# First tap and silu of the latents' convolutions: from VectorE and an exp/ln sigmoid to ScalarE and tanh

## The chip, the cores and the metric

The kernel runs on one core of one Trainium2 chip. The metric is the device time of one execution in microseconds (us). Three runs of the kernel before took 3646.48, 3650.38 and 3652.74 us; their median is 3650.38 us. Five engines work beside each other, each through its own queue in order: TensorE (PE for matmuls, PEld for its weight loads), VectorE (DVE), ScalarE (ACT), GpSimd (POOL), and SyncE (SP), whose queue issues most DMAs. An instruction that waits for a semaphore holds up everything that stands behind it in its queue.

## What is computed

The program is two blocks one after the other on a sequence of 1024 tokens of width 1024: a first block of two layers (dilated attention with a gated scan, then a second gated scan), and a second block with a hybrid mixer and an expert layer. The change lies in the hybrid mixer of the second block, on its 1024 latent tokens. What matters of the reference:

```
def dwconv_centred(u, w):          # width 5, one filter per channel
    ...
def ssd_stream(z, xbc, ...):
    xbc = jax.nn.silu(dwconv_centred(xbc, conv_w) + conv_b)
    ...
    y = y.reshape(b, T, SSD_DIM) * jax.nn.silu(z)
    return rms_norm(y, norm_g), s_f, s_b

def gdn_stream(qkv, gate, ...):
    qkv = jax.nn.silu(dwconv_centred(qkv, conv_w))
    q, k, v = ...
    q = l2_norm(q) * (GDN_HEAD_DIM ** -0.5)
    k = l2_norm(k)
    ...
    o = rms_norm(o_f + flip_t(o_b), norm_g) * jax.nn.silu(gate)
```

So there are 16 blocks of 128 channels that are projected, convolved and put through silu: three each of k, q and v (the delta rule, "gdn", in column-major token order), and seven of xbc (the state-space branch, "ssd", which alone has a bias). k and q are normalised per head afterwards. Six more blocks are gates: projected and put through silu, without a convolution. The same code also handles 256 context tokens earlier in the program, with `lat` false.

## The kernel before

The latents' stage (`latent_mixers`) holds 128 channels on the partitions and 1024 tokens along the free dimension. For each block, `Projections.dense` loads the weights, splits them into a high and a low part (`whi` by ACT, L115, and `wlo` by POOL, L116) and multiplies in two halves of 512 tokens, 24 matmuls each (`mm3`, L139 to L141), into one of three PSUM banks `mm`.

`Projections.conv` then does, for each of the 16 blocks: two copies from PSUM into the padded tile `cu` (ACT, L1134 or L1137); the first tap (DVE, L1141, or L1143 with the bias); four more taps (DVE, L1145); the silu as `sigmoid` (L612 exp on ACT, L613 a clamp on DVE, L614 ln and L615 exp on ACT) and a product (DVE, L1148). The sigmoid is written over `cu`. For q and k there follow a square (ACT, L1150), a sum over each head by a matmul (L1153), and per half a scale (DVE, L1156), ln and exp (ACT, L1157 and L1158) and a product (DVE, L1159). At last the result `cacc` is stored by a DMA that SP issues (L1160). `cu`, `cacc` and the scale `cr` have two buffers each, so the first tap of a block waits until the block two before has been stored.

`Projections.gate` does the six gate blocks with `silu_from`: exp, clamp, ln, exp and a product on each half of 512 tokens, straight from PSUM.

Beside this runs `gdn_inverse`, three generators (one for each pair of heads) that invert triangular matrices. Its core is a recursion of 31 steps of two DVE instructions each (`gtmp` L1465 and `gTT` L1466), a POOL copy (`gN`, L1470), DMAs through DRAM, and small matmuls (`a`, L1504 to L1514). The loop over the blocks draws four steps of it after each block. Three k blocks come first, then q and v alternately, then the seven xbc blocks x0 to x6, the six gates, and a pooling branch (`pu`). When the last inverse is stored, the next stage (the two scans) begins with loads on SP (L1228 to L1595).

The order of instructions on each engine is not written out by hand: the tile framework schedules them by a timeline of its own, so an edit in one place can move instructions for some way behind it.

The activation functions of ACT come in table sets. The program loads one at its start (L43, a set with exp and ln), and one more at L2073 in the expert layer, where it already uses tanh; the tool that builds the program puts an ACT_TABLE_LOAD ahead of an instruction whose function the loaded set lacks.

Of the kernel before, what the change touches and what calls it, by code (L numbers as in the profile page):

```python
# [13 lines left out]
AF = mybir.ActivationFunctionType  # L14
ALU = mybir.AluOpType
# [1055 lines left out]
class Projections:  # L1071
# [4 lines left out]
    def __init__(self, g, pool, n, X, lat, out):  # L1076
        self.g, self.pool, self.n, self.X, self.lat, self.out = g, pool, n, X, lat, out
        self.tmp = pool
        self.step = min(512, n)
        nc, I = g.nc, g.I  # L1080
        self.gw = pool.tile([P, 9, 5], F32, name="gcw", tag="gcw", bufs=1)
        nc.sync.dma_start(self.gw, I["gdn_cw"])
        self.sw = pool.tile([P, 7, 5], F32, name="scw", tag="scw", bufs=1)
        nc.sync.dma_start(self.sw, I["ssd_cw"])
        self.sb = pool.tile([P, 7], F32, name="scb", tag="scb", bufs=1)
        nc.sync.dma_start(self.sb, I["ssd_cb"])

    def dense(self, b, put):

# [34 lines left out]
    def conv(self, b, cw, bias, dst, colmajor, normed=None):  # L1124
        g, nc, n, step, pool = self.g, self.g.nc, self.n, self.step, self.tmp
        nb = 2 if self.lat else 1
        u = pool.tile([P, n + 4], F32, name="cu", tag="cu", bufs=nb)
        nc.vector.memset(u[:, 0:2], 0.0)
        nc.vector.memset(u[:, n + 2:n + 4], 0.0)

        def put(t0, ps):
            if colmajor:
                r0 = t0 // 64
                nc.scalar.copy(u[:, 2:2 + n].rearrange("p (c r) -> p r c", r=16)[:, r0:r0 + step // 64, :],  # L1134
                               ps.rearrange("p (r c) -> p r c", c=64))
            else:
                nc.scalar.copy(u[:, 2 + t0:2 + t0 + step], ps)  # L1137
        self.dense(b, put)
        acc = pool.tile([P, n], F32, name="cacc", tag="cacc", bufs=nb)
        if bias is None:  # L1140
            nc.vector.tensor_scalar(acc, u[:, 0:n], cw[:, 0:1], None, op0=ALU.mult)  # L1141
        else:
            nc.vector.tensor_scalar(acc, u[:, 0:n], cw[:, 0:1], bias, op0=ALU.mult, op1=ALU.add)  # L1143
        for i in range(1, 5):
            nc.vector.scalar_tensor_tensor(acc, u[:, i:i + n], cw[:, i:i + 1], acc, op0=ALU.mult, op1=ALU.add)  # L1145
        sg = u[:, :n]
        sigmoid(g, sg, acc)
        nc.vector.tensor_mul(acc, acc, sg)  # L1148
        if normed is not None:
            nc.scalar.activation(sg, acc, AF.Square)  # L1150
            for t0 in range(0, n, step):
                ps = g.psum("tr")
                nc.tensor.matmul(ps[:, :step], g.blockones, sg[:, t0:t0 + step], start=True, stop=True)  # L1153
                r = pool.tile([P, step], F32, name="cr", tag="cr", bufs=nb)
                s2 = normed ** -2
                nc.vector.tensor_scalar(r, ps[:, :step], s2, EPS2 * s2, op0=ALU.mult, op1=ALU.add)  # L1156
                nc.scalar.activation(r, r, AF.Ln)  # L1157
                nc.scalar.activation(r, r, AF.Exp, scale=-0.5)  # L1158
                nc.vector.tensor_mul(acc[:, t0:t0 + step], acc[:, t0:t0 + step], r)  # L1159
        nc.sync.dma_start(dst, acc)  # L1160
# [13 lines left out]
    def gate(self, b, dst):  # L1174

        def put(t0, ps):
            zt = self.tmp.tile([P, 512], F32, name="zt", tag="zt", bufs=2)
            silu_from(self.g, self.tmp, zt, ps)
            self.g.nc.sync.dma_start(dst[:, t0:t0 + 512], zt)
        self.dense(b, put)  # L1180

# [36 lines left out]
def ssd(g, pool, n, xbcz, rows, s0, fin=None, Y=None):  # L1218


    nc, I = g.nc, g.I
# [71 lines left out]
    def outputs(c, xb, old):  # L1293

        cs = slice(c * P, (c + 1) * P)
        BC = pool.tile([P, 7, P], F32, name="sBC", tag="sBC", bufs=2)
        nc.sync.dma_start(BC, xbcz[3:10].rearrange("c p t -> p c t")[:, :, cs])
        cb = g.psum("mm")
        for gr in range(2):
            nc.tensor.matmul(cb[:, gr * P:(gr + 1) * P], BC[:, gr], BC[:, 2 + gr], start=True, stop=True)  # L1300
        E = []
        for d in range(2):
            row = pool.tile([P, 6, P], F32, name=f"srow{d}", tag=f"srow{d}", bufs=2)
            nc.sync.dma_start(row, dap(rows.dram, [[0, P], [n, 6], [1, P]], (32 * d + 6) * n + c * P))
            nc.vector.tensor_sub(row, row, col[:, d, c, :, None].to_broadcast([P, 6, P]))

            s = 1 if d == 0 else -1
            nc.gpsimd.affine_select(row, row, pattern=[[0, 6], [s, P]], compare_op=ALU.is_ge, fill=NEG, base=0,
                                    channel_multiplier=-s)
            nc.scalar.activation(row, row, AF.Exp)  # L1310
            E.append(row)
        M = E[0]
        nc.gpsimd.tensor_tensor(M, M, E[1], op=ALU.add)
        m4 = M.rearrange("p (g h) t -> p g h t", g=2)
        with g.up():
            nc.vector.tensor_mul(m4, m4, cb[:, :256].rearrange("p (g t) -> p g t", g=2)[:, :, None, :].to_broadcast([P, 2, 3, P]))
        zt = g.psum("mm")
        for i in range(3):
            nc.tensor.transpose(zt[:, i * P:(i + 1) * P], BC[:, 4 + i], g.ident)
        sz = pool.tile([P, 384], F32, name="sz", tag="sz", bufs=2)  # L1320
        with g.up():
            nc.scalar.copy(sz, zt[:, :384])
        xd = pool.tile([P, 384], F32, name="sxd", tag="sxd", bufs=2)
        nc.gpsimd.tensor_tensor(six(xd), six(xb[:, :384]), bc(dsk), op=ALU.mult)
        ti = [pool.tile([P, 384], F32, name=f"sti{d}", tag=f"sti{d}", bufs=2) for d in range(2)]
        for d, S in ((0, old), (1, Sb[c])):
            yi = g.psum("mm")
            for gr in range(2):
                nc.tensor.matmul(yi[:, gr * 192:(gr + 1) * 192], BC[:, 2 + gr], S[:, gr * 192:(gr + 1) * 192],
                                 start=True, stop=True)  # L1330
            with g.up():
                nc.vector.tensor_mul(six(ti[d]), six(yi[:, :384]), bc(W[:, d, 1, c]))
            nc.gpsimd.tensor_tensor(xd, xd, ti[d], op=ALU.add)
        y = g.psum("mm")
        for h in range(6):
            hs = slice(h * 64, h * 64 + 64)
            nc.tensor.matmul(y[:, hs], M[:, h], xb[:, hs], start=True, stop=True)
        yt = ti[0]
        with g.up():
            nc.vector.tensor_add(yt, xd, y[:, :384])  # L1340
        nc.vector.tensor_mul(yt, yt, sz)
        rs = rms_rstd(g, pool, yt, 384, junk=xd)
        nc.scalar.activation(yt, yt, AF.Copy, scale=rs)
        return yt
# [382 lines left out]
def gdn_finish(g, pool, O, hp, gate, Y):  # L1727

    nc = g.nc
    ncp = 8  # L1730
    sq = pool.tile([P, ncp * 2, 64], F32, name="fsq", tag="hx", bufs=2)
    o3 = O.rearrange("p c h v -> p (c h) v")
    nc.scalar.activation(sq, o3, AF.Square)
    ss = pool.tile([P, ncp * 2], F32, name="fss", tag="fss", bufs=2)
    nc.vector.tensor_reduce(ss, sq, axis=AX.X, op=ALU.add)
    nc.gpsimd.tensor_scalar(ss, ss, 1.0 / 64, EPS2, op0=ALU.mult, op1=ALU.add)
    nc.gpsimd.tensor_tensor(ss, ss, g.mh[:, :16], op=ALU.pow)
    nc.vector.tensor_mul(o3, o3, ss[:, :, None].to_broadcast([P, ncp * 2, 64]))
    gt = pool.tile([P, T], F32, name="fg", tag="hx", bufs=2)
    nc.sync.dma_start(gt, gate)  # L1740
    for c0 in range(0, ncp, 4):
        tr = g.psum("a")
        for i in range(4):
            nc.tensor.transpose(tr[:, i * P:(i + 1) * P], O[:, c0 + i].rearrange("p h v -> p (h v)"), g.ident)

        g3 = gt.rearrange("p (r c) -> p r c", c=64)[:, :, c0 * 8:c0 * 8 + 32]
        nc.vector.tensor_mul(g3, tr.rearrange("p (c r) -> p r c", r=16), g3)
    hi = pool.tile([P, T], F32R, name="fhi", tag="hx", bufs=2)
    for hf in range(2):
        hs = slice(hf * 512, (hf + 1) * 512)  # L1750
        g.split(hi[:, hs], gt[:, hs].bitcast(F32R), gt[:, hs])
        for i, part in enumerate((hi.bitcast(F32), gt)):
            nc.sync.dma_start(Y[5 + hp][i][:, hs], part[:, hs])
# [702 lines left out]
```

## Time and profile before

| | |
|---|---|
| median of three runs | 3650.38 us (3646.48 to 3652.74) |
| the profiled execution | 3659.12 us, of which the span of the profile is 3656.9 us |
| busy: PE, DVE, ACT, POOL | 3228.8, 2576.0, 1595.0, 1439.0 us |
| mean granted TensorE clock | 0.935 |

The profiled execution is one run, 8.7 us above the median; its span runs from the first to the last instruction. Busy time is the time in which an engine has at least one instruction under way. PE's busy time is modelled at its ends, so that a fully busy PE is not PE at its peak. The granted clock is given as a share of full speed. The latents' convolutions lie between about 2413 and 2670 us of the span, the gates behind them up to 2727 us, and the next stage begins at about 2775 us.

### The profile page before, as it was taken

How to read it: one execution, taken by the hardware profiler on the slowest of the kernel's cores; microseconds unless marked ns; L12 is line 12 of the kernel's file. 1: busy time of each engine (PE TensorE's matmuls, PEld its weight loads, DVE VectorE, ACT ScalarE, POOL GpSimd, SP SyncE). 2: the span in 40 equal slices, each digit the busy share in tenths (PEclk: the TensorE clock that was granted, in tenths of full speed). 3: DMA queues.
4: the chain of work that ended last, by engine and by line, in shares of the span. 5: the costliest groups of instructions: out<-in, count | busy, mean ns of one | idle time of the engine just before them, and what ended most of it. 6: DMA issues, size and time to landing. Idle time of an engine off the chain costs nothing.

```text
span 3656.9 us, 63623 instructions
## 1 busy us (share of the span) xinstructions
PE 3228.8 (88%) x23752; PEld 2610.4 (71%) x23752; DVE 2576.0 (70%) x5604; ACT 1595.0 (44%) x3332; POOL 1439.0 (39%) x1431
## 2 busy tenths in 40 slices
PE   7998898999979999999999989688896878858887
PEld 6887776766658787878787867566675766636665
DVE  4776664346675777976868686779994765678887
ACT  3444434544324545455545441344433331235665
POOL 4657773000041333433334321723214563345553
PEclk9999999999989999999999999789997888969999
DMA  5223244253242211111112135234337655768994
GB/s 181 82 87 102 87 140 137 74 177 99 96 153 73 70 64 53 58 54 40 56 45 76 54 126 174 77 82 133 104 108 187 140 135 205 211 219 295 312 332 148
DMA packets 374001, 461.28 MB, mean 126 GB/s; under 512 B 150419, under 2 KB 280723, under 8 KB 373692
## 3 DMA queue, kind: packets, MB, share of 16 engines
q1 hardware_dynamic: 359852, 407.93, 36.1%
q0 software_dynamic: 13840, 49.29, 4.4%
q8 instruction: 187, 3.06, 0.4%
q14 instruction: 122, 1.00, 0.1%
HBM read 357.57 MB, written 104.27 MB: 126 GB/s over the span
## 4 chain that ended last, share of the span: by engine, by line
PE 46%; DVE 23%; DMA 9%; issue 9%; POOL 8%; ACT 3%; SPq 2%; DVEq 0%; POOLq 0%; ACTq 0%
PE mm L139 9%; PE mm L140 9%; PE mm L141 9%; PE a L249 2%; POOL aw L966 2%; DVE cacc L1145 2%; DVE elo L2025 2%; DMA srow<-rdsl 1%; DMA aw<-in_ada_w_dram 1%; PE a L406 1%; PE o L225 1%; POOL wlo L116 1%; DVE gtmp L1465 1%; PE a L141 1%; DVE u_kb L187 1%
## 5 line engine op out<-in xcount | busy, mean ns | idle before, releaser
L116 POOL TENSOR_TENSOR wlo<-wraw,whi 128x1024 fp32r<-128x1024 f32 (+1 forms) x131 | 328.2, 2509 | 528.1 <-ACT whi L115 517.7
L2023 ACT CAST ehi<-eraw 128x1024 fp32r<-128x1024 f32 x192 | 200.4, 1050 | 144.5 <-PE a L141 100.7
L139 PE MATMUL mm<-x1h,whi 128*128 128x512 f32 x576 | 235.4, 409 | 3.3 <-DVE G L921 1.7
L140 PE MATMUL mm<-x1l,whi 128*128 128x512 f32 x576 | 233.9, 406 | 1.8 <-DVE x1l L133 1.8
L141 PE MATMUL mm<-x1h,wlo 128*128 128x512 f32 x576 | 233.8, 406 | 0.0
L139 PE MATMUL mm<-whi,x1h 128*128 128x256 f32 x768 | 221.8, 289 | 0.4 <-DVE G L921 0.4
L2025 DVE TENSOR_TENSOR elo<-eraw,ehi 128x1024 fp32r<-128x1024 f32 x138 | 196.8, 1460 | 35.7 <-ACT ehi L2023 34.2
L141 PE MATMUL mm<-whi,x1l 128*128 128x256 f32 x768 | 219.6, 286 | 0.0
L140 PE MATMUL mm<-wlo,x1h 128*128 128x256 f32 x768 | 219.1, 286 | 0.0
L115 ACT CAST whi<-wraw 128x1024 fp32r<-128x1024 f32 (+1 forms) x131 | 136.0, 1040 | 158.0 <-PE mm L140 78.5
L2027 POOL TENSOR_TENSOR elo<-eraw,ehi 128x1024 fp32r<-128x1024 f32 x54 | 138.9, 2577 | 161.9 <-ACT ehi L2023 144.1
L140 PE MATMUL mm<-wlo,xh 128*128 128x256 f32 x640 | 185.5, 290 | 1.9 <-POOL wlo L116 1.9
L141 PE MATMUL mm<-whi,xl 128*128 128x256 f32 x640 | 185.5, 290 | 0.0
L139 PE MATMUL mm<-whi,xh 128*128 128x256 f32 x640 | 184.8, 290 | 0.0
L139 PE MATMUL mm<-x2h,whi 128*128 128x512 f32 x400 | 168.2, 420 | 10.2 <-ACT cu L1134 5.7
L139 PE MATMUL mm<-whi,yin 128*128 128x512 f32 x352 | 150.2, 430 | 23.4 <-DVE z L824 14.1
L141 PE MATMUL mm<-x2h,wlo 128*128 128x512 f32 x400 | 164.9, 413 | 0.8 <-POOL wlo L116 0.8
L140 PE MATMUL mm<-x2l,whi 128*128 128x512 f32 x400 | 164.9, 412 | 0.0
L966 POOL TENSOR_SCALAR aw<-aw,ac 128x128 f32<-128x128 f32 x256 | 123.7, 498 | 85.5 <-DMA aw<-in_ada_w_dram 51.9
L139 PE MATMUL mm<-xh,whi 128*128 128x512 f32 x336 | 137.6, 410 | 20.0 <-ACT whi L115 16.7
L139 PEld LDWEIGHTS mm<-whi,x1h 128*128 128x128 f32 x768 | 146.8, 191 | 3.1 <-issue 1.0
L140 PEld LDWEIGHTS mm<-wlo,x1h 128*128 128x128 f32 x768 | 146.8, 191 | 0.6
(742 smaller groups left out, 10437.4 us busy)
## 6 DMA issues: line engine op xcount, KB each, us to landing
eraw<-in_we_gate_dram SPq DMA_DIRECT2D x64, 512.0 KB
eraw<-in_we_up_dram SPq DMA_DIRECT2D x64, 512.0 KB
eraw<-in_we_down_dram SPq DMA_DIRECT2D x64, 512.0 KB
yin<-yd POOLq DMA_DIRECT2D x29, 1024.0 KB, 9.7
aw<-in_ada_w_dram SPq DMA_DIRECT2D x96, 256.0 KB
yd<-y_hl SPq DMA_DIRECT2D x80, 256.0 KB
wraw<-in_w_dram SPq DMA_DIRECT2D x25, 512.0 KB
wraw<-in_w_out_dram SPq DMA_DIRECT2D x24, 512.0 KB
```

The source lines that it names most:

```text
L115: nc.scalar.copy(hi[:, :sz], raw[:, :sz])
L116: nc.gpsimd.tensor_tensor(lo[:, :sz], raw[:, :sz], hi[:, :sz].bitcast(F32), op=ALU.subtract)
L139: nc.tensor.matmul(ps, sh, mh, start=first and i == 0, stop=False)
L140: nc.tensor.matmul(ps, sh, ml, start=False, stop=False)
L141: nc.tensor.matmul(ps, sl, mh, start=False, stop=last and i == n - 1)
L187: nc.vector.tensor_sub(c32(kb), bc[:, :, il:il + 1].to_broadcast([P, nck, 32]), bc)
L249: nc.tensor.matmul(ap[32 * c:32 * c + 32, o + lo:o + hi], sta[:, o + 32 * c:o + 32 * c + 32], mov[:, o + lo:o + hi], start=True, stop=True)
L966: nc.gpsimd.tensor_scalar(w[:, k], w[:, k], at(k), 0.0, op0=ALU.mult, op1=ALU.add)
L1145: nc.vector.scalar_tensor_tensor(acc, u[:, i:i + n], cw[:, i:i + 1], acc, op0=ALU.mult, op1=ALU.add)
L2023: nc.scalar.copy(hi, raw)
L2025: nc.vector.tensor_sub(lo, raw, hi.bitcast(F32))
L2027: nc.gpsimd.tensor_tensor(lo, raw, hi.bitcast(F32), op=ALU.subtract)
```

## The change

For the latents only (`lat` true), three things are done. The first tap moves from DVE to ACT, as an activation with a scale of one value for each partition (and the bias, for xbc). The silu is rewritten: with h = x/2, silu(x) is h (1 + tanh h). The convolution's weights and bias are multiplied by 0.5 once (three small DVE instructions, L1090 of the changed kernel), so that the accumulator is h already; then one tanh on ACT and one combined instruction on DVE, (tanh + 1) times h, replace exp, clamp, ln, exp and the product. The gates do the same from PSUM with a scale of 0.5 in the activation, and their result is twice the silu; the two places that use them (`sz` and `g3`) multiply by 0.5 in an instruction that was there before.

```
@@ Projections.__init__
+        if lat:
+            for t in (self.gw, self.sw, self.sb):
+                nc.vector.tensor_scalar(t, t, 0.5, None, op0=ALU.mult)
@@ Projections.conv
-        if bias is None:
+        if self.lat:
+            if bias is None:
+                nc.scalar.activation(acc, u[:, 0:n], AF.Copy, scale=cw[:, 0:1])
+            else:
+                nc.scalar.activation(acc, u[:, 0:n], AF.Identity, scale=cw[:, 0:1], bias=bias)
+        elif bias is None:
             nc.vector.tensor_scalar(acc, u[:, 0:n], cw[:, 0:1], None, op0=ALU.mult)
         else:
             nc.vector.tensor_scalar(acc, u[:, 0:n], cw[:, 0:1], bias, op0=ALU.mult, op1=ALU.add)
         for i in range(1, 5):
             nc.vector.scalar_tensor_tensor(acc, u[:, i:i + n], cw[:, i:i + 1], acc, op0=ALU.mult, op1=ALU.add)
         sg = u[:, :n]
-        sigmoid(g, sg, acc)
-        nc.vector.tensor_mul(acc, acc, sg)
+        if self.lat:
+            nc.scalar.activation(sg, acc, AF.Tanh)
+            nc.vector.scalar_tensor_tensor(acc, sg, 1.0, acc, op0=ALU.add, op1=ALU.mult)
+        else:
+            sigmoid(g, sg, acc)
+            nc.vector.tensor_mul(acc, acc, sg)
@@ Projections.gate
-            silu_from(self.g, self.tmp, zt, ps)
+            self.g.nc.scalar.activation(zt, ps, AF.Tanh, scale=0.5)
+            self.g.nc.vector.scalar_tensor_tensor(zt, zt, 1.0, ps, op0=ALU.add, op1=ALU.mult)
@@ ssd, outputs
-            nc.scalar.copy(sz, zt[:, :384])
+            nc.scalar.mul(sz, zt[:, :384], 0.5)
@@ gdn_finish
-        nc.vector.tensor_mul(g3, tr.rearrange("p (c r) -> p r c", r=16), g3)
+        nc.vector.scalar_tensor_tensor(g3, g3, 0.5, tr.rearrange("p (c r) -> p r c", r=16), op0=ALU.mult, op1=ALU.mult)
```

The order of the instructions is the same as before up to the first latent convolution and differs from there on. Three places follow. In the changed kernel the lines of `conv` are L1146 and L1148 (first tap), L1154 (taps), L1157 (tanh), L1158 (product), L1163 (square), L1169 to L1172 (normalisation).

ACT, at the first two k blocks (`cu_27136` and `cacc_27197` are the first, `cu_27224` and `cacc_27285` the second, `cr_27211` and `cr_27218` the halves' scales of the first), before:

```order
L612 ACTIVATE cu_27136<-cacc_27197 128x1024
L115 CAST whi_27886<-wraw_27885 128x1024
L614 ACTIVATE cu_27136<-cu_27136 128x1024
L1134 COPY cu_27224<-mm_27259 128x8x64
L615 ACTIVATE cu_27136<-cu_27136 128x1024
L1150 ACTIVATE cu_27136<-cacc_27197 128x1024
L612 ACTIVATE cu_27224<-cacc_27285 128x1024
L115 CAST whi_27975<-wraw_27974 128x1024
L614 ACTIVATE cu_27224<-cu_27224 128x1024
L1157 ACTIVATE cr_27211<-cr_27211 128x512
```

and in the changed kernel (the first block is `cu_27139` and `cacc_27200` there, and the second's accumulator is written by ACT):

```order
L1146 ACTIVATE cacc_27200<-cu_27139,gcw_26962 128x1024
L1157 ACT_TABLE_LOAD
L1157 ACTIVATE cu_27139<-cacc_27200 128x1024
L115 CAST whi_27877<-wraw_27876 128x1024
L1138 COPY cu_27224<-mm_27259 128x8x64
L1163 ACTIVATE cu_27139<-cacc_27200 128x1024
L1146 ACTIVATE cacc_27285<-cu_27224,gcw_26962 128x1024
L1170 ACT_TABLE_LOAD
L1170 ACTIVATE cr_27211<-cr_27211 128x512
L1138 COPY cu_27309<-mm_27318 128x8x64
L1171 ACT_TABLE_LOAD
L1171 ACTIVATE cr_27211<-cr_27211 128x512
```

The first taps have come onto this queue, three instructions of each sigmoid have become one, and the ln (L1170) and the exp (L1171) of the normalisation each have a table load ahead of them. Over the stage there are 21 such loads: one at the first tanh, ten ahead of an L1170 and ten ahead of an L1171; two more stand in the next stage (at L1256 and L1262), and the one that stood at L2073 is gone.

ACT, at the normalisation of the last q block (`cr_28323` and `cr_28330` before, `cr_28302` and `cr_28309` after), before:

```order
L1157 ACTIVATE cr_28323<-cr_28323 128x512
L1137 COPY cu_28617<-mm_28626 128x512
L1158 ACTIVATE cr_28323<-cr_28323 128x512
L1157 ACTIVATE cr_28330<-cr_28330 128x512
L1158 ACTIVATE cr_28330<-cr_28330 128x512
```

and in the changed kernel:

```order
L1170 ACT_TABLE_LOAD
L1170 ACTIVATE cr_28302<-cr_28302 128x512
L1171 ACT_TABLE_LOAD
L1171 ACTIVATE cr_28302<-cr_28302 128x512
L1170 ACT_TABLE_LOAD
L1170 ACTIVATE cr_28309<-cr_28309 128x512
L1171 ACT_TABLE_LOAD
L1171 ACTIVATE cr_28309<-cr_28309 128x512
L1157 ACTIVATE cu_28418<-cacc_28479 128x1024
```

Where ln and exp alternate between the halves there are four loads for a block, where both ln come first there are two.

DVE, at the first xbc blocks (`cacc_28589` is x0 and `cacc_28678` x1 before; `gtmp` and `gTT` belong to the inverse), before:

```order
L1143 TENSOR_SCALAR cacc_28678<-cu_28617,scw_26964,scb_26966 128x1024
L1145 SCALAR_TENSOR_TENSOR cacc_28589<-cu_28528,scw_26964,cacc_28589 128x1024
L1465 TENSOR_TENSOR gtmp_27862<-gTT_27861,gN_27860 128x676
L1145 SCALAR_TENSOR_TENSOR cacc_28678<-cu_28617,scw_26964,cacc_28678 128x1024
L1145 SCALAR_TENSOR_TENSOR cacc_28589<-cu_28528,scw_26964,cacc_28589 128x1024
L1466 TENSOR_REDUCE gTT_27861<-gtmp_27862 128x26
L1145 SCALAR_TENSOR_TENSOR cacc_28678<-cu_28617,scw_26964,cacc_28678 128x1024
L1465 TENSOR_TENSOR gtmp_27862<-gTT_27861,gN_27860 128x729
L613 TENSOR_SCALAR cu_28528<-cu_28528 128x1024
```

and in the changed kernel (x0 is `cacc_28565`, x1 `cacc_28651`):

```order
L1154 SCALAR_TENSOR_TENSOR cacc_28565<-cu_28504,scw_26964,cacc_28565 128x1024
L1479 TENSOR_TENSOR gtmp_27853<-gTT_27852,gN_27851 128x676
L1154 SCALAR_TENSOR_TENSOR cacc_28565<-cu_28504,scw_26964,cacc_28565 128x1024
L1480 TENSOR_REDUCE gTT_27852<-gtmp_27853 128x26
L1154 SCALAR_TENSOR_TENSOR cacc_28651<-cu_28590,scw_26964,cacc_28651 128x1024
L1479 TENSOR_TENSOR gtmp_27853<-gTT_27852,gN_27851 128x729
L1158 SCALAR_TENSOR_TENSOR cacc_28565<-cu_28504,cacc_28565 128x1024
```

The first tap and the clamp have left this queue, and the product of a block stands where its clamp stood. The steps of the recursion keep their place beside the same blocks.

## Rows read from the trace of the kernel before

**Rows 1.** Windows: stretch, us, busy PE, PEld, DVE, ACT, POOL (instructions), clock, DMA share, GB/s.

```profile
2414.00:2477.00 63.00, 62.89 (x353) 48.25 (x354) 45.19 (x51) 34.87 (x43) 12.32 (x5) 0.95 0.28 83
2477.00:2640.00 163.00, 141.44 (x860) 109.48 (x859) 158.17 (x207) 68.80 (x80) 51.82 (x26) 0.90 0.43 120
2640.00:2743.00 103.00, 103.00 (x728) 82.19 (x726) 96.86 (x147) 44.01 (x64) 20.63 (x15) 1.00 0.32 106
2743.00:2776.00 33.00, 25.83 (x332) 19.93 (x329) 14.85 (x23) 9.56 (x17) 7.68 (x7) 0.73 0.55 168
```

**Rows 2.** Timeline of DVE, k blocks: start, duration, idle before and releaser.

```profile
2444.50 0.75 DVE L1141 TENSOR_SCALAR cacc<-cu,gcw 128x1024 f32<-128x1024 f32 x1 [2.70 <-DMA lk<-cacc]
...
2458.66 0.75 DVE L1141 TENSOR_SCALAR cacc<-cu,gcw 128x1024 f32<-128x1024 f32 x1 [2.60 <-DMA lk<-cacc]
...
2477.12 0.75 DVE L1141 TENSOR_SCALAR cacc<-cu,gcw 128x1024 f32<-128x1024 f32 x1 [0.99 <-DMA lk<-cacc]
```

**Rows 3.** Chain of waits, the k blocks' stores: start and length in us.

```profile
2441.84 2.57 DMA lk<-cacc
...
2454.88 3.68 DMA lk<-cacc
```

**Rows 4.** By line, DVE in the latents' stage: count, duration ns min/median/max, starts.

```profile
L1141 DVE TENSOR_SCALAR cacc<-cu,gcw x9: 745/753/2894, 2415.0 to 2537.9; 128x1024 f32<-128x1024 f32 x9
...
L1143 DVE TENSOR_SCALAR cacc<-cu,scw,scb x7: 801/809/2509, 2569.0 to 2650.4; 128x1024 f32<-128x1024 f32 x7
...
L613 DVE TENSOR_SCALAR cu<-cu x16: 677/680/1691, 2422.2 to 2664.2; 128x1024 f32<-128x1024 f32 x16
...
L613 DVE TENSOR_SCALAR sg<-sg x12: 412/419/2626, 2655.3 to 2724.9; 128x512 f32<-128x512 f32 x12
...
L1145 DVE SCALAR_TENSOR_TENSOR cacc<-cu,scw,cacc x28: 1265/1274/3442, 2571.0 to 2658.2; 128x1024 f32<-128x1024 f32 x28
...
L1148 DVE TENSOR_TENSOR cacc<-cacc,cu x16: 1210/1217/1629, 2427.9 to 2667.9; 128x1024 f32<-128x1024 f32 x16
```

**Rows 5.** Timeline of DVE: a first tap, a clamp, and what follows each.

```profile
2496.57 0.75 DVE L1141 TENSOR_SCALAR cacc<-cu,gcw 128x1024 f32<-128x1024 f32 x1
2497.24 0.16 DVE L1466 TENSOR_REDUCE gTT<-gtmp 128x3 f32<-128x9 f32 x1
...
2520.03 0.68 DVE L613 TENSOR_SCALAR cu<-cu 128x1024 f32<-128x1024 f32 x1
2520.63 0.28 DVE L1465 TENSOR_TENSOR gtmp<-gTT,gN 128x121 f32<-128x121 f32 x1
```

**Rows 6.** By line, ACT: count, duration ns min/median/max, first and last start.

```profile
L612 ACT ACTIVATE cu<-cacc x16: 1040/1060/1065, 2421.1 to 2661.6; 128x1024 f32<-128x1024 f32 x16
...
L1157 ACT ACTIVATE cr<-cr x12: 608/630/653, 2436.0 to 2567.6; 128x512 f32<-128x512 f32 x12
...
L855 ACT ACTIVATE z<-z,bnm,brs x16: 1226/1241/1246, 1052.8 to 2342.9; 128x1024 f32<-128x1024 f32 x16
```

**Rows 7.** Timeline of ACT around the one table load inside the program.

```profile
3252.93 1.05 ACT L2023 CAST ehi<-eraw 128x1024 fp32r<-128x1024 f32 x1 [0.66 <-PE a L141]
3254.00 1.28 ACT L2073 ACT_TABLE_LOAD   x1
3255.30 0.60 ACT L2073 ACTIVATE hid<-a 128x512 f32<-128x512 f32 x1
```

**Rows 8.** Timeline of ACT and DVE at the first q block's normalisation.

```profile
2485.72 1.23 ACT L1157 ACTIVATE cr<-cr 128x512 f32<-128x512 f32 x2 [3.15 <-DVE cr L1156]
2486.86 1.14 ACT L1158 ACTIVATE cr<-cr 128x512 f32<-128x512 f32 x2
...
2488.56 2.22 DVE L1159 TENSOR_TENSOR cacc<-cacc,cr 128x512 f32<-128x512 f32 x2
```

**Rows 9.** Timelines of DVE and SP: the last recursion step, last inverse's store.

```profile
2742.57 1.15 DVE L1466 TENSOR_REDUCE gTT<-gtmp 128x31 f32<-128x961 f32 x1
...
2775.25 0.34 SPq L1518 DMA_DIRECT2D gT<-gR  x1
```

## The prediction

> **What bounds the kernel now.** I read the windows first, cut where the latents' stage changes its character, then the timelines of DVE and ACT inside it, then the chain of waits, and last the prices by line. The windows [rows 1] show four stretches that follow each other without a gap. From 2414 to 2477 us (the k blocks) PE is busy 62.9 of 63 us and DVE only 45.2: here DVE waits. Its timeline [rows 2] says for what: each first tap sits idle for 2.70, 2.60 and 0.99 us until the store of the block two before (`DMA lk<-cacc`) has landed, because `cacc` has two buffers; the chain of waits puts 2.57 and 3.68 us on two such stores [rows 3]. From 2477 to 2640 us DVE is busy 158.2 of 163 us, PE only 141.4 at a granted clock of 0.90, ACT 68.8 [rows 1]: DVE is the bound, and its queue holds convolutions and the recursion of the inverse mixed. From 2640 to 2743 us PE is busy all 103 us at a clock of 1.00, DVE 96.9 [rows 1]: the gates' projections. From 2743 us, when the last recursion step ends, to the store of the last inverse at 2775.25 us [rows 9], a chain of small matmuls and DMAs runs with nothing full. SP then starts the next stage, since its loads stand behind that store in its queue. So a microsecond saved in the second stretch should reach the end; in the others it should not by itself.
>
> **The change part by part.** Each number is for the profiled execution (3659.1 us); the result is set against the median of 3650.4, 8.7 us lower, on the ground that the stage itself has no reason to differ by more than a share of this.
>
> *First tap off DVE.* It costs 0.753 us without a bias (nine blocks) and 0.809 with one (seven) [rows 4]. The timeline shows the next instruction starting 0.67 us after a tap and 0.60 after a clamp of 0.68 [rows 5], so in a packed queue I take durations less 0.08. In the DVE-bound stretch five taps of the first kind start (v0 to v2, q1, q2) and six of the second (x0 to x5): 5 x 0.67 + 6 x 0.73 = 7.7 us.
>
> *Clamp off DVE.* Nine clamps fall in that stretch: 9 x 0.60 = 5.4 us.
>
> *Product.* The plain product (1.217) becomes a combined instruction like the taps' (1.274) [rows 4]: nine times 0.06 more, 0.5 us. The three halvings of small weights come before the first block and are put at nothing; DVE waits there.
>
> Sum on DVE in the second stretch: 7.7 + 5.4 - 0.5 = **12.6 us less**. The k blocks and q0 also lose taps and clamps, about 5 us, but in a stretch where DVE waits for stores: 0. The last xbc blocks and the twelve clamps of the gates (0.419 each [rows 4], 5.0 us) lie where PE is full: 0. If PE were not the bound there, they would be worth up to 7 us more.
>
> *ACT's arithmetic.* A sigmoid there is three passes of 1.06 us [rows 6]; now one tanh of the same shape, and a first tap. The trace has no tap on ACT; it has a pass with a scale and a bias for each partition on the same shape, 1.241 us (L855), and a plain one, 1.060 [rows 6], so a tap lies between. Per block ACT gets 2.12 us less and 1.06 to 1.24 more. ACT is busy 69 of 163 us, so neither counts; what counts is the latency of one block. The chain exp, clamp, ln, exp (3.2 + 0.7 us) becomes 1.06, and a tap of 0.75 becomes 1.24: 2.3 us shorter per block.
>
> *Table loads.* The profile has a load at L2073: 1.28 us, the pass before it ends 0.02 us ahead and the tanh starts 0.02 us behind it [rows 7]. The changed kernel has 21 in this stage. The one ahead of an ln carries no wait of its own and can run while ACT waits for DVE, as ACT did for 3.15 us at q0 [rows 8]. The one between ln and exp stands in the chain. The k and q blocks have 4, 2, 4, 4, 2, 4 loads. With one hidden in each, 3, 1, 3, 3, 1, 3 stand in the chain: 9 us in the k blocks and 9 us in the q blocks. In the k blocks the shorter silu gives back 3 x 2.3 = 7 us, and the loop is set by the stores, so I put them at 0, with ±3 for the range. In the q blocks DVE has other work to run in between: before, the products of q0 started 0.56 us after its exps had ended (2486.86 + 1.14 against 2488.56 [rows 8]), and in the new order taps and recursion steps stand between scale and product in q1 and q2, but only a tap in q0. I take half as exposed: **4.5 us more**. The bounds are 0 and all ten loads, 12.8.
>
> *The first tap's wait.* It now waits for the store on ACT, not on DVE. Behind it on ACT stand the copies that free PSUM banks and the casts `whi` on which POOL's `wlo`, and so PE, depend. PE had 3 banks and was full in that stretch; I cost it at nothing, since before the change the same copies waited for the same blocks' `cu`. Without that cover it would be the 2.6 us of [rows 2] per block.
>
> *Gates and the places that halve.* `sz` and `g3` keep their instructions, 0. The two loads at the start of the next stage (2.6 us) lie beside its DMA loads, 0; the one at L2073 goes, at most 1.3 us, 0.
>
> *Order behind the stage.* The loads of the next stage start in another order. I can't price that from the trace and allow ±5 us.
>
> Sum: -12.6 + 4.5 = -8.1, and about 1 us more because PE, waiting less in the second stretch, should hold its clock above 0.90 there: **-9 us**, 3650.4 - 9 = **3641 us**. About 0.2% (7.3 us) is what a measurement of this kernel can tell from no change.
>
> A rule of the Trainium skill speaks against the change ("ScalarE: Activation LUTs", What ACT_TABLE_LOAD costs, and Table sets): functions should be batched by set, and a switch costs about 2.66 us, a load of 1283 ns and a drain of 1380. The trace agrees with the load and shows no drain behind or before it, at its one load. By the page the exposed part would be 9.3 us in place of 4.5 and the sum about -4 us.
>
> **The rivals.**
>
> *The loads are exposed, and it gets slower.* The place is the loop of the k and q blocks: ACT is in order, so a load delays what stands behind it too, the copies for PE and the next tap. All 20 loads exposed are 25.7 us; less the 12.6 that gives +13, about 3661. It decides against the change beyond 12.6 + 7.3 = 19.9 us, which is 3.3 us for each of the six blocks. For it: by the count above 14 of the 20 stand in a block's chain, and the order was planned as if they took no time. Against it: ACT is busy 55% of the first and 42% of the second stretch [rows 1], DVE and stores already make it wait, and the silu is 2.3 us shorter per block. Chance 0.14. A switch of twice the row's price, at the exposure of my sum, would give -12.6 + 9 - 1, about -5; that it is dearer here than at L2073 I hold for unlikely, 0.04, which is counted with the next case.
>
> *DVE's time is not on the path.* PE works 141 of 163 us in the second stretch and then 103 without a pause. If PE can't run ahead, because it waits for copies on ACT or the reordered normalisation sums, then the relief stays inside the stage: the sum of -12.6 shrinks by the exposed loads and what PE adds, to -4 to +4, about 3649. For it: PE's idle time in the stretch is only 21.6 us, part of it at a low clock. Chance 0.34 (this is the case of no measurable change).
>
> *More than counted.* The gates' and last blocks' 7 us count as well, since the recursion that ends last runs on DVE (its last step ends at 2743.7 [rows 9], when PE is nearly done), and the loads hide: -12.6 - 7 - 1 = -20, about 3630. For it: DVE is at 94% in the third stretch. Against: PE at 100%. Chance 0.14.
>
> **How the numbers follow.** My forecast, -7.3 to -14 us, gets 0.38; with the larger gain that makes 0.52 for faster, 0.34 for no change, 0.14 for slower. The likeliest case's own range is 3636 to 3643. The range for 8 in 10 takes in most of the larger gain and of the no-change case and the ±5 of the next stage: 3628 to 3657.
>
> **What would show it.** Right: the DVE-bound stretch some 8 us shorter with DVE still above 90%; table loads of about 1.28 us with ACT waiting around them; L1172 products waiting a few us in all for L1171; the gates' stretch as long as now with PE full; the store of the last inverse about 9 us earlier, and the rest of the program shifted as a whole. Wrong: k blocks spaced wider than the 14.2 us between the taps at 2444.50 and 2458.66 [rows 2]; PE idle on `mm` for copies of `cu`; loads followed by an idle ACT of more than a microsecond; or a next stage that takes back the gain.

## The result and the profile after

The changed kernel is slower: 3673.90 us (median of seven runs, 3662.07 to 3678.55) against 3650.38 us (seven runs, 3637.47 to 3652.74); the ratio of the runs is 1.0062, with a 95% interval of 1.0043 to 1.0080. The prediction was 3641 us, range 3628 to 3657: wrong in sign. Of all runs in this document one, of the kernel e7 below, took 9721.14 us; it counts in that kernel's median, not in its ratio. The profiled execution took 3678.55 us (span 3676.5, clock 0.930).

The stage that was changed did become faster. Three marks cut the trace: the last store of the previous stage (`x2d<-z`), the last inverse's store (`gT<-gR`, which ends the latents' stage) and the first store of the router's input (`h2d<-h`). Timeline by tile, before: count, duration in ns, first and last start in us.

```profile
L2247 SPq DMA_DIRECT2D x2d<-z x8: 319/320/327, 2291.9 to 2354.3; - x8
L1518 SPq DMA_DIRECT2D gT<-gR x6: 319/328/344, 2638.9 to 2775.2; - x6
L2202 SPq DMA_DIRECT2D h2d<-h x8: 319/320/6528, 3149.0 to 3197.9; - x8
```

The same of after:

```profile
L2261 SPq DMA_DIRECT2D x2d<-z x8: 319/320/327, 2294.1 to 2358.5; - x8
L1532 SPq DMA_DIRECT2D gT<-gR x6: 319/319/338, 2643.6 to 2767.6; - x6
L2216 SPq DMA_DIRECT2D h2d<-h x8: 319/320/6513, 3170.3 to 3219.2; - x8
```

The reader is to take differences, since work that is the same in both already ended 4.2 us later in this run. The stage took 2775.2 - 2354.3 = 420.9 us before and 409.1 after: **11.8 us gained**. From the last inverse to the first `h2d` store it was 373.8 us and is 402.7: **28.9 us lost**, in code that the diff touches only at `sz` and `g3`. Behind the first `h2d` store both need 506 to 508 us.

Inside the stage, windows of after with the cuts of [rows 1] (which lie 4.2 us earlier against the work here), in the same columns:

```profile
2414.00:2477.00 63.00, 54.71 (x285) 40.70 (x286) 35.64 (x46) 47.55 (x52) 9.82 (x7) 0.91 0.21 66
2477.00:2640.00 163.00, 151.86 (x958) 117.75 (x956) 150.23 (x199) 77.27 (x85) 53.44 (x27) 0.95 0.47 129
2640.00:2743.00 103.00, 101.34 (x740) 80.75 (x737) 87.08 (x123) 24.69 (x37) 22.26 (x17) 0.97 0.39 122
2743.00:2776.00 33.00, 26.87 (x305) 20.26 (x304) 14.73 (x20) 8.83 (x16) 6.42 (x8) 0.73 0.47 145
```

DVE is less busy in each of the first three, 27 us in all, PE is busier in the second (151.9 for 141.4 us) at a higher clock (0.95 for 0.90), but less busy in the first (54.7 for 62.9). What answers to [rows 9], DVE's last recursion steps and SP's last inverse store:

```profile
2725.47 1.16 DVE L1479 TENSOR_TENSOR gtmp<-gTT,gN 128x961 f32<-128x961 f32 x1
2726.67 1.16 DVE L1480 TENSOR_REDUCE gTT<-gtmp 128x31 f32<-128x961 f32 x1
...
2767.59 0.32 SPq L1532 DMA_DIRECT2D gT<-gR  x1
```

The last recursion step is 20.1 us earlier against the `x2d` mark (368.2 us behind it, before 388.3), but the tail from it to the store is 8.2 us longer (40.9 for 32.7): by the windows PE is busy 101.3 of 103 us where the small matmuls of the last inverse now begin, among the pooling branch's. No run tested that. And the table loads show as waits on DVE. ACT, the normalisation of the first q block, q0 (start, duration):

```profile
2479.71 1.28 ACT L1170 ACT_TABLE_LOAD   x1
2481.01 0.63 ACT L1170 ACTIVATE cr<-cr 128x512 f32<-128x512 f32 x1
2481.65 1.28 ACT L1171 ACT_TABLE_LOAD   x1
2482.95 0.63 ACT L1171 ACTIVATE cr<-cr 128x512 f32<-128x512 f32 x1
...
2486.84 0.63 ACT L1171 ACTIVATE cr<-cr 128x512 f32<-128x512 f32 x1
```

The second half goes like the first: four loads stand in a row, 5.1 of 7.8 us, and nothing else is on ACT. DVE waits for the end of each pair. Lines of DVE in the stage, before and then after: busy, mean ns, idle before them and for whom.

```profile
L1159 DVE TENSOR_TENSOR cacc<-cacc,cr 128x512 f32<-128x512 f32 x12 | 9.7, 834 | 2.0 <-ACT cr L1158 2.0
L1141 DVE TENSOR_SCALAR cacc<-cu,gcw 128x1024 f32<-128x1024 f32 x9 | 9.4, 1049 | 10.9 <-DMA lk<-cacc 6.3 <-ACT cu L1134 4.6
```

```profile
L1154 DVE SCALAR_TENSOR_TENSOR cacc<-cu,gcw,cacc 128x1024 f32<-128x1024 f32 x36 | 49.9, 1385 | 14.5 <-ACT cacc L1146 14.1
...
L1172 DVE TENSOR_TENSOR cacc<-cacc,cr 128x512 f32<-128x512 f32 x12 | 8.1, 688 | 12.4 <-ACT cr L1171 12.4
```

The products wait 12.4 us for the exp where they waited 2.0. The taps behind the first wait 14.1 us for ACT; the first taps of k, q and v waited 10.9 before.

Now the loss. The output projection splits its weights (`mraw`, in chunks of 256 KB) for four groups; the experts' weights (`eraw`, 512 KB each) come behind on the same SP queue. SP before:

```profile
3112.67 4.57 SPq L1895 DMA_DIRECT2D mraw<-in_w_out_dram  x4
3117.28 0.91 SPq L2022 DMA_DIRECT2D eraw<-in_we_gate_dram  x2
```

SP after:

```profile
3111.33 1.05 SPq L1909 DMA_DIRECT2D mraw<-in_w_out_dram  x2
3112.43 0.91 SPq L2036 DMA_DIRECT2D eraw<-in_we_gate_dram  x2
3113.38 0.43 SPq L2036 DMA_DIRECT2D eraw<-in_we_up_dram  x1
3113.91 0.38 SPq L1909 DMA_DIRECT2D mraw<-in_w_out_dram  x1
...
3125.47 1.93 SPq L2036 DMA_DIRECT2D eraw<-in_we_up_dram  x2
3129.82 2.92 SPq L1909 DMA_DIRECT2D mraw<-in_w_out_dram  x2
```

Fourteen expert loads, 7.3 MB, now stand ahead of the last two weight loads. The chain of waits of after shows what that costs:

```profile
3118.10 11.66 DMA eraw<-in_we_up_dram
3129.82 12.91 DMA mraw<-in_w_out_dram
3142.82 0.59 DVE mraw L1910
```

The last weight is there at 3142.8 us, and the matmuls of the last group wait for it. Before, the chain went through one `mraw` load of 5.54 us and was back on DVE at 3118.23 us.

### The profile page after: what moved, and what is told of

It is laid out like the page before. It is cut to its first block, busy times and chain, and to the rows that moved or that the text cites. A ratio compares the mean times of both kernels' runs of the same rounds, so it can differ in the third digit from the quotient of the medians.

```text
span 3676.5 us, 63596 instructions
## 1 busy us (share of the span) xinstructions
PE 3244.1 (88%) x23752; PEld 2620.7 (71%) x23752; DVE 2562.0 (70%) x5563; ACT 1595.5 (43%) x3314; POOL 1427.3 (39%) x1431
## 4 chain that ended last, share of the span: by engine, by line
PE 43%; DVE 24%; DMA 10%; issue 9%; POOL 8%; ACT 4%; SPq 2%; DVEq 0%; POOLq 0%; ACTq 0%
PE mm L139 9%; PE mm L140 8%; PE mm L141 8%; DVE cacc L1154 2%; DVE elo L2039 2%; PE a L249 2%; POOL aw L966 2%; DVE gtmp L1479 2%; DMA aw<-in_ada_w_dram 1%; PE a L406 1%; DMA srow<-rdsl 1%; PE o L225 1%; DVE gTT L1480 1%; POOL wlo L116 1%; DVE u_kb L187 1%
```

## The experiments

Theory **O**: the stage gained, and the scheduler's new order behind it lost 29 us, above all through those weight loads. Rival **L**: the table loads and the taps on ScalarE cost the time, and the order is innocent. The 5,661 instructions behind the stage are the same in both kernels but for the operations of `sz` and `g3` (and the table loads, two more at the start of the scans and one less in the experts); only their order on the five engines differs. So orders can be exchanged: a kernel records where the stage ends, and at its end gets issue-order edges (no waits) between the later instructions of each engine, in a recorded order.

| kernel | stage | to first `h2d` | sum | median us | ratio to before, interval |
|---|---|---|---|---|---|
| before | 420.9 | 373.8 | 794.7 | 3650.38 | |
| after | 409.1 | 402.7 | 811.8 | 3673.90 | 1.0062 (1.0043 to 1.0080) |
| e1 after, old order | 406.1 | 377.7 | 783.8 | 3641.82 | 0.9991 (0.9977 to 1.0004) |
| e2 before, new order | 419.7 | 401.3 | 821.0 | 3682.59 | 1.0080 (1.0056 to 1.0103) |
| e3 after, weights first | 406.2 | 385.5 | 791.7 | 3652.17 | 1.0005 (0.9992 to 1.0018) |
| e4 tap alone, old order | 413.1 | 375.7 | 788.8 | 3645.48 | 0.9995 (0.9982 to 1.0008) |
| e5 scans alone in old order | 407.3 | 403.5 | 810.8 | 3669.22 | 1.0044 (1.0031 to 1.0057) |
| e6 tanh alone, old order | 411.2 | 376.2 | 787.4 | 3644.42 | 0.9985 (0.9976 to 0.9994) |
| e7 one ln, old order | 398.2 | 380.5 | 778.7 | 3637.64 | 0.9966 (0.9953 to 0.9979) |
| e8 20 more loads, old order | 406.3 | 383.4 | 789.7 | 3641.15 | 0.9978 (0.9969 to 0.9988) |
| e9 e7 with 12 more loads | 422.2 | 378.7 | 800.9 | 3658.60 | 1.0024 (1.0014 to 1.0034) |
| e10 before with one ln | 423.5 | 370.3 | 793.8 | 3648.92 | 1.0007 (0.9992 to 1.0021) |
| e11 e1 again | 406.0 | 380.3 | 786.3 | 3642.14 | 0.9989 (0.9976 to 1.0002) |
| e12 one ln, weights first | 398.6 | 372.8 | 771.4 | 3633.22 | 0.9957 (0.9943 to 0.9971) |

The first three columns come from the three marks of each profiled execution, in us; the medians are of all runs of that kernel, and the runs of before that they were compared with have medians of 3647.2 to 3649.0. The code of the stage is the same in after, e1, e3, e5 and e11, and these span 3.1 us; a difference of that size in one column can be chance.

**e1 and e2: the orders exchanged.**

```
@@ latent_mixers, behind the last inverse
+    g.mark = g.nc.cur_bb.bb.instructions[-1].name
@@ end of body
+    keep_order(g)
+def keep_order(g):
+    late = ...                       # all that was written behind g.mark
+    for k in ORDER:                  # recorded: engine by engine
+        i = late[int(k)]
+        if i.engine in last:
+            g.tc.add_manual_dep(i, last[i.engine].name, <NoSync>, reason="order")
+        last[i.engine] = i
```

> The changed kernel, but behind the latents' stage every engine issues its 5,661 later instructions in the order that they have in the kernel before. Theory O (the stage itself gained about 8 us, and the new order behind it lost about 29): about 8 us faster than the kernel before, some 3642 us, ratio 0.998; the last inverse stored near 2768 us, the first h2d store near 3141 us. Rival L (the table loads and the taps on ScalarE cost the time, the order is innocent): as slow as the changed kernel, about 3672 us, ratio 1.006.

> The other way round: the kernel before, with the instructions behind the latents' stage in the order of the changed kernel. O: about 29 us slower than the kernel before, some 3679 us, ratio 1.008, although nothing in the computation differs; the last inverse stored near 2775 us as before, the first h2d store near 3178 us. L: no difference, 3650 us, ratio 1.000.

Timeline by tile of e1 and then of e2, the last two marks:

```profile
L1532 SPq DMA_DIRECT2D gT<-gR x6: 320/323/371, 2632.3 to 2753.2; - x6
L2217 SPq DMA_DIRECT2D h2d<-h x8: 319/320/6415, 3130.9 to 3179.7; - x8
```

```profile
L1518 SPq DMA_DIRECT2D gT<-gR x6: 319/329/344, 2642.8 to 2778.3; - x6
L2203 SPq DMA_DIRECT2D h2d<-h x8: 319/320/6391, 3179.6 to 3228.4; - x8
```

Each segment follows what O says it hangs on: the stage the code (406.1 and 419.7 us), the part behind it the order (377.7 and 401.3). The old arithmetic in the new order is 0.8% slower, about 29 us, which is all that was lost, and its chain of waits goes through the same place as that of after: an `eraw` load of 13.67 us and then an `mraw` load of 11.91. The new arithmetic in the old order is no slower than before. L, which expected 1.006 and 1.000, falls.

**e3: the weight loads alone.**

```
@@ MixersOut.group
-                nc.sync.dma_start(raw, g.I["w_out2"][:, c, hs])
+                g.last_w[c] = nc.sync.dma_start(raw, g.I["w_out2"][:, c, hs])
@@ experts.units
+            with g.tc.issue_after(g.last_w[6].ins):
-            nc.sync.dma_start(raw..., blk[...])
+                nc.sync.dma_start(raw..., blk[...])
```

> The changed kernel with its own order, except that the experts' weight loads (eraw) are queued on SP behind the last load of the output projection's weights (mraw of group 3). If O is right and these loads are the place: the 24.6 us between 3118 and 3143 us in the chain of waits shrink to the 6 us that they took before, so 18 to 25 us less than the changed kernel, 3649 to 3656 us, ratio 1.000 to 1.0015. If O is right but the loss is spread over the scans' stores: at most half of that, 3660 to 3670 us. L: unchanged, about 3672 us.

SP of e3, around the last weight loads:

```profile
3090.06 15.17 SPq L1910 DMA_DIRECT2D mraw<-in_w_out_dram  x6
3105.28 0.92 SPq L2038 DMA_DIRECT2D eraw<-in_we_gate_dram  x2
```

The edge hangs on the last load of chunk 6 of 0 to 7; in the trace all sixteen `mraw` loads stand ahead of the first `eraw`. This order on one queue takes 21.7 us off the changed kernel's median, and 402.7 us behind the stage become 385.5. So most of the loss lies there. What is left against e1 (385.5 for 378 to 380) goes with the scans' order: the last of their `shl` stores starts 256.4 us behind the last inverse, in e1 244.3, and in e12, which has e3's edge too, 247.3 (372.8 to the first `h2d`). No run exchanges the scans' order alone with the weights ahead.

**e5: the scans alone in the old order**, with the edges of e1 for the 2,148 instructions ahead of the output projection and, apart from these, the new order for the rest.

> The changed kernel with the scans (all that is written between the last inverse and the output projection) in the order of the kernel before, and the output projection, the router and the experts in the order of the changed kernel. If the loss has two places, late scan stores (about 10 us) and weight loads behind expert loads (about 20 us), only the first comes back: the last inverse to the first h2d store takes 392 to 398 us (374 to 378 in the old order, 401 to 403 in the new one), some 3660 us, ratio 1.003 to 1.005. If the weight loads fall behind only because the scans end late: all comes back, about 376 us and ratio 0.998 to 0.999.

That expectation failed: nothing came back (403.5 us). The chain of waits of e5:

```profile
3099.26 7.08 DMA eraw<-in_we_gate_dram
3106.36 15.28 DMA eraw<-in_we_up_dram
3121.70 9.48 DMA mraw<-in_w_out_dram
```

The scans' last stores were earlier (246.7 us behind the inverse, 264.2 in after), but the last weight still stands behind the expert loads, and lands 782.6 us behind the `x2d` mark, in after 784.2. The two losses don't add: while the weights are late, late scans are free.

**e4 and e6: the two halves of the change**, both with the old order behind the stage.

```
@@ e4: conv of the kernel before
+        if self.lat:
+            nc.scalar.activation(acc, u[:, 0:n], AF.Copy or AF.Identity, scale=cw[:, 0:1], ...)
@@ e6: conv of the changed kernel
-        if self.lat:
-            nc.scalar.activation(acc, u[:, 0:n], ...)
```

> The kernel before with the first tap on ScalarE alone (exp, ln, exp sigmoid kept, no weights halved, no table loads added), and the order of the kernel before behind the stage. By the term of the prediction (11 taps off a full VectorE, 0.67 and 0.73 us each): 7.7 us faster, 3643 us, ratio 0.998. If VectorE's time is not on the path: no difference. If taps waiting on ScalarE hold up the copies behind them: slower, up to 2.6 us a block or 40 us.

> The changed kernel with the first tap back on VectorE (tanh, halved weights and table loads stay), old order behind the stage. From the last x2d store to the last inverse store the kernel before takes 420 us, the tap alone 413, the whole change 406 to 409. By the prediction's terms (clamp 5.4 and product -0.5 off VectorE, 4.5 of exposed loads on): about 420, no gain. If the loads are hidden: 415. If they are all exposed: 428. Time: ratio 0.9985 to 1.000.

The tap alone is worth 7.8 us of stage (term: 7.7). Tanh alone is worth 9.7, where my terms gave about nothing; that expectation failed. Together they give 12 to 15, less than the sum. By their timed ratios e4 can't be told from no change (0.9982 to 1.0008), e6 is just below it (0.9976 to 0.9994).

**e8, e7, e9, e10: what a table load costs.** e8 puts loads where ACT waits anyway; e7 takes 9 of 20 out of the normalisation's chain; e9 puts 12 back in; e10 makes e7's edit without any loads.

```
@@ e8: conv, behind the tanh, if not normed
+                nc.scalar.activation(extra, sg[:, 0:1], AF.Ln, scale=0.0, bias=1.0)
@@ e7, e10: conv, for both halves (r is one tile of 1024)
+            if self.lat:
+                nc.scalar.activation(r, r, AF.Ln)
+                nc.scalar.activation(r, r, AF.Exp, scale=-0.5)
+                nc.vector.tensor_mul(acc, acc, r)
@@ e9: between that ln and that exp
+                nc.scalar.activation(extra[:, 0:1], r[:, 0:1], AF.Tanh)
+                nc.scalar.activation(extra[:, 1:2], extra[:, 0:1], AF.Ln, scale=0.0, bias=1.0)
```

> The changed kernel, old order behind the stage, with an ln of one column behind each tanh of the v and xbc blocks (its result is used nowhere): 20 more table loads of 1.28 us, 25.7 us of ScalarE, and ten tiny passes. If loads beside a waiting ScalarE cost nothing: the stage as in the whole change, 406 to 410 us. If half are exposed: 420. If all are: 433, and some 26 us more than the changed kernel with the old order.

> The changed kernel, old order behind the stage, with one scale tile of 1024 for both halves of a k or q block: one ln, one exp and one product in place of two each, so 11 table loads of the normalisation in place of 20. If the loads are half exposed, as the prediction took: 4 to 6 us less for the stage than the 406 to 409 of the whole change. If they are hidden: 0 to 2 us more, since the first half waits for the second. Time: ratio 0.997 to 0.9995.

> The kernel with one ln and one exp for a k or q block (stage 398 us in place of 406), with a tanh and an ln of one column put between them, so that each block has four table loads in a row again. The last ln gives the exp a bias of 0. If it was the loads in this chain that cost the 8 us: about 407 us with half of the 12 added loads (15.4 us) and tiny passes exposed, up to 416 with all. If it was the merging (fewer passes and waits): 398 to 400.

> The kernel before (its sigmoid and its first tap, no table loads in the stage), old order behind the stage, with one scale tile, one ln, one exp and one product for both halves of a k or q block. If the loads were the cost in the changed kernel: stage 419 to 422 us as before. If the merging is what helps: 411 to 414 us, ratio 0.998.

ACT of e8, at an xbc block:

```profile
2599.38 1.28 ACT L1157 ACT_TABLE_LOAD   x1
2603.72 1.06 ACT L1157 ACTIVATE cu<-cacc 128x1024 f32<-128x1024 f32 x1 [3.05 <-DVE cacc L1154]
...
2605.93 1.28 ACT L1160 ACT_TABLE_LOAD   x1
2607.22 0.20 ACT L1160 ACTIVATE extra<-cu 128x1 f32<-128x1 f32 x1
```

The load runs at once and the tanh then waits another 3.05 us for DVE: 20 more loads leave the stage at 406.3 us (e1 406.1). In the chain it is otherwise. DVE's product of e7 and then of e9, the idle time ahead of it:

```profile
L1181 DVE TENSOR_TENSOR cacc<-cacc,cr 128x1024 f32<-128x1024 f32 x6 | 8.3, 1376 | 6.7 <-ACT cr L1180 6.5
```

```profile
L1184 DVE TENSOR_TENSOR cacc<-cacc,cr 128x1024 f32<-128x1024 f32 x6 | 7.4, 1226 | 28.6 <-ACT cr L1183 28.6
```

Twelve loads there (15.4 us, and 12 passes of 0.20) cost 24.0 us of stage, and DVE waits 22 us longer; nine fewer gave 8. Both are more than expected (407 to 416 us for e9, 4 to 6 us for e7). By the last stores of the k and of the q blocks, 14.8 us of the 24 fall in the k blocks and 8.7 in the q blocks. Six loads and six passes, the share of either, are 8.9: in the q blocks they are exposed in full, in the k blocks something else comes on top. In e9's first k block ACT runs a cast, a square and a copy for 2.9 us between the third and the fourth load; what makes up the rest was not tested. e10 shows that the merging by itself gives nothing (423.5 us, before 420.9).

**e11 and e12.**

> The changed kernel with the old order behind the stage, a second time, since its first ratio (0.9977 to 1.0004) could not tell a gain from none, while the same kernel with 20 more table loads came out at 0.9969 to 0.9988. If the stage's gain of 12 to 14 us reaches the end less the 4 us that the scans seemed to give back: ratio 0.9975 to 0.998, 3640 to 3642 us. If it is given back: 1.000.

> A version without any imposed order: the changed kernel with one ln and one exp for a k or q block (as e7) and the experts' loads queued behind the last mraw load (as e3); the scans are in the order that the scheduler then chooses. The stage should take 398 us as in e7. If the scans' order costs what it did in e3 (first h2d store some 8 us later than in the old order): ratio 0.998 to 0.9995, 3641 to 3646 us. If it doesn't: 0.9965, 3636 us.

e11 gives e1's result again, with an upper end of the interval at 1.0002. e12 joins e7's edit and e3's and imposes no other order; it has the lowest median, 15.7 us under the kernel before in the same series (3633.22 for 3648.87). Its scans did not cost what they did in e3, the second case of its expectation (0.9965).

## Why the prediction was wrong

**The step that failed** is "Order behind the stage. The loads of the next stage start in another order. I can't price that from the trace and allow ±5 us", entered as 0. It cost 29 us (e2), three times the rest of the sum. "A next stage that takes back the gain" stood among the signs of being wrong, but no rival and no chance went with it. The reordering was in sight: the orders differ from the first latent convolution on, and SP's alone shows the last `mraw` loads behind fourteen `eraw` loads. An estimate of its price was also at hand, from the bytes ahead in the queue and the rate in the window of before where those loads run (last column, GB/s):

```profile
3112.00:3132.00 20.00, 16.16 (x69) 13.37 (x70) 13.41 (x24) 2.48 (x4) 5.58 (x4) 0.89 1.08 320
```

7.3 MB at 320 GB/s are 23 us; e3 gave back 21.7 us of the median and 17.2 of the stretch between the marks. I looked only at the start of the next stage, where little changed, and not on to the next place where a transfer is waited for.

**Right.** *ACT's tap* between 1.06 and 1.24 us: 1.143 without a bias, 1.244 with one. *The first tap's wait* at nothing: DVE's 14.1 us for the ACT tap stand for the 10.9 that its own first taps waited before. *PE's clock* in the second stretch: 0.95 for 0.90. *The loads at the next stage's start* at nothing: behind the stage e4, which lacks them, takes 375.7 us, and e6, which has them, 376.2, no more apart than two profiles of one kernel (e1 377.7, e11 380.3). The rival of exposed loads, which alone stood for a slower kernel, was not the reason: e1 has every load and is not slower than before. (Its sum has a slip: 3650.4 + 13 is about 3663, not 3661.)

**Right in part by luck.** *First tap off DVE*: 7.7 us, measured 7.8 (e4). But in e4 the last store of the k blocks comes 4.2 us later behind the `x2d` mark than before (124.1 for 119.9), the last convolution's store 8.0 us earlier (306.8 for 314.8), the last recursion step 12.6 us earlier, and the tail behind it is 4.8 us longer. So the stretch for which the term was made gained some 12 us, and the k blocks gave back 4.2.

**Mis-sized.** *Table loads*, 4.5 us for half of those in the q blocks' chains, 0 for the k blocks. The products' wait for the exp grew by 12.4 - 2.0 = 10.4 us in all. In the q blocks it is 4.8 us (none before): 3.5 in q0, where only a tap stands between scale and product, none in q1 and 1.2 in q2, where taps and recursion steps stand between. DVE at the products of q0, q1 and the second one of q2:

```profile
2483.61 0.69 DVE L1172 TENSOR_TENSOR cacc<-cacc,cr 128x512 f32<-128x512 f32 x1 [1.54 <-ACT cr L1171]
2487.50 0.69 DVE L1172 TENSOR_TENSOR cacc<-cacc,cr 128x512 f32<-128x512 f32 x1 [2.00 <-ACT cr L1171]
...
2524.80 1.28 DVE L1172 TENSOR_TENSOR cacc<-cacc,cr 128x512 f32<-128x512 f32 x2
...
2561.57 0.69 DVE L1172 TENSOR_TENSOR cacc<-cacc,cr 128x512 f32<-128x512 f32 x1 [1.23 <-ACT cr L1171]
```

So in the q blocks the size of the term and its ground, that DVE has other work to run in between, held by this measure. What was too small is the 0 of the k blocks: the other 7.6 us of the wait lie there (2.0 before), and e7, with nine fewer loads in both, ends the k blocks 3.5 us and the stage 8 us earlier than e1. The Trainium skill ("ScalarE: Activation LUTs", What ACT_TABLE_LOAD costs) would add a drain of 1380 ns to each load; the rows of after and of e9 show none, the pass behind a load starts 0.01 to 0.02 us after it.

*The second stretch*, -8.1 us. The last stores of the k blocks and of the xbc convolutions, before and then after:

```profile
L1160 SPq DMA_DIRECT2D lk<-cacc x3: 319/327/338, 2441.8 to 2474.2; - x3
L1160 SPq DMA_DIRECT2D lx<-cacc x7: 319/320/338, 2592.2 to 2669.1; - x7
```

```profile
L1173 SPq DMA_DIRECT2D lk<-cacc x3: 326/327/337, 2446.1 to 2475.7; - x3
L1173 SPq DMA_DIRECT2D lx<-cacc x7: 319/327/338, 2584.4 to 2656.5; - x7
```

Against the `x2d` mark the k blocks end 2.7 us earlier (117.2 for 119.9) and the convolutions 16.8 (298.0 for 314.8), so the q, v and xbc blocks gave 14.1 us, 6 more than the sum. The same code in e1, e3, e5 and e11 has these marks at 116.8 to 117.1 and 297.3 to 298.2, the kernel before in e2 at 119.3 and 314.4. From there to the last recursion step it is 3.3 us less (6.0 in e1), a stretch that I had put at 0. Together these are 20.1 us, the size of the case "more than counted" (-20, chance 0.14), but that case had the loads hidden, and in the q blocks they were not. Why the q, v and xbc blocks gave 6 us more than counted, no run separates. The tail behind the last step then gave back 8.2 us, for which no term stood. The stage's own sum of -8 was so 4 to 7 us too small (-11.8 in after, -14.8 in e1).

**What stays open.** With the old order the stage's 14.8 us reach the first `h2d` store as 8 to 11 us (e1, e11), and the timed gain is 3 to 6 us (by ratios and by medians), 0.1% with an interval that touches 1. A shorter stage mostly goes with a longer stretch behind it (370.3 us behind a stage of 423.5, 380.5 behind one of 398.2), as if part of the scans did not start from the last inverse; that was not tested. Beyond the `h2d` store single profiles differ by several us at the same code (503 us to the end in e1, 496 in e11), and the rest may be no more than that.

## What to carry to other kernels

Where a scheduler orders the program, an edit has two effects, and the second can be larger: compare the orders to the end of the program, look for each place where a small load that is waited for has fallen behind large prefetches on the same queue, and price it by the bytes ahead of it. Then pin such an order with an edge, so that edits elsewhere can be measured by themselves. A table load cost nothing ahead of an instruction that waited (e8); in a chain that another engine waits for it cost its full time once that engine had run out of work ahead of the waiting instruction (the q blocks of e9), and no wait where there was enough of it (q1 of after).

## What the runs showed that I had not expected

The order of the same instructions alone moved this kernel by 0.8% (e2), more than the arithmetic that it carries. DMA moved 352 GB/s from 3112 to 3132 us of after, and a weight load of 256 KB queued behind 7.3 MB ended 12.91 us after its issue, with 5.54 us for one ahead of them. A table load took 1.28 us wherever it stood, the next pass began 0.01 to 0.02 us behind it unless it had to wait for another engine, and a load ahead of an ACT instruction that waited for DVE ran during the wait.
